# Tap matrices loaded instead of built, state rows moved whole, and idle products of ones in TensorE's planned waits

## The chip, the core and the metric

One core of a Trainium2 chip runs the program. The metric is the time of one execution in microseconds on the device; three runs of the kernel before are shown, and one further execution was profiled. An engine is called by its letters in the profile: PE is TensorE (PEld its weight loads), DVE VectorE, ACT ScalarE, POOL GpSimd, SP SyncE, which issues all DMA transfers of this kernel.

## What is computed

Two layers of a streaming encoder for 576 frames: 512 of a new stream and 64 of a running one with caches. Cut to what the change touches:

```
def trunk_layer(x, conv_state, k_past, v_past, ki_past, ...):
    h = x @ w_in
    a, g, q, k, v, qi, ki, wi = jnp.split(h, points, axis=-1)
    u = a * jax.nn.sigmoid(g)
    conv_out, new_conv = conv_mixer(u, conv_state, ...)
    ...
    mix = jnp.concatenate([conv_out, attn_out], axis=-1) @ w_o
    x = layer_norm(ALPHA * x + mix, ln1_g, ln1_b)
    gate, up = jnp.split(x @ w_gate_up, 2, axis=-1)
    x = layer_norm(ALPHA * x + (jax.nn.silu(gate) * up) @ w_down, ln2_g, ln2_b)
    return x, k, v, ki, new_conv
```

`conv_mixer` is a depthwise convolution of 31 taps with a layer norm and silu behind it; between it and the end come rope, indexer scores, a top-k and attention. `new_conv` is the last 30 rows of the convolution's input; they are an output (`conv_p` for the new stream, `conv_s` for the running one), and the rows of the running stream before it (`state_conv`) are an input.

## The kernel before, in words

The program is not written in the order in which it runs. Every operation is recorded by a `Plan` (lines 175 to 251) with a priority, an estimated cost and what it depends on. `schedule` (253 to 350) lays the operations out over the five engines by these costs, always the most urgent that can start; a tile gets a place in its pool when its first operation is laid out, and for some tags (`IN_TURN`, 156, `tap` and the wide PSUM tag `w` among them) in the order of recording. `issue` (352 to 362) then emits the list; each engine executes its part strictly in that order and waits where data is late. All instructions are emitted from line 362, so the profile shows that line for nearly all of them, and rows are told apart by the names of the tiles.

A layer begins with the input projection `w_in` in 18 tiles of 512 KB. A weight tile is loaded into `raw` (two buffers), split into two parts `whi` (ScalarE) and `wlo` (VectorE or GpSimd), and each product is made of three matmuls (`prod`). Rope sends its rows through DMA to exchange halves (`rope_s<-rope_h`).

The convolution works on four chunks of 128 channels. `glu` (720 to 735) writes the gated input of a chunk into `u`, eight phases of 80 columns; the four columns of state per phase come by a DMA from `st` (723), and the last columns of either stream go out by two DMAs straight from `u` (731, 732): runs of four floats. `convolve` (654 to 677) sends `u` to DRAM (`ud`) and back as `v` with another arrangement of partitions. Then, for each of eight phases, GpSimd builds a tap matrix `taps` of 128 x 640 from an identity (`eyes`) and the taps (`wv`), two buffers (664 to 667), and TensorE makes five float32 products of 76 columns with it (669 to 671); a float32 product shows as two instructions. The result is in a `wide` PSUM tile of two banks, of which there is one; VectorE reads it in two halves into `y` (673 to 676). The same wide tile takes the shift of the convolution's norm, the sums and spreads of all norms (`Moments`, 489 to 524) and the logits of the 64 running frames (926).

Indexer scores (`dots`), top-k on VectorE (`m`, `sel`) and attention (`qk`, `pp`, `po`) are interleaved with the convolution. Then follow `w_o` with a norm, and SwiGLU in four parts, where a Strassen-like scheme of seven products (`Seven`, 1076 to 1149) takes most tiles; its sums `s3`, `s4` use the tag `tap` too.

Of the kernel before, what the change touches and what calls it, by code (L numbers as in the profile page):

```python
# [49 lines left out]
PH = 8  # L50
# [7 lines left out]
CWID = PH * COUT  # L58

# [112 lines left out]
HOP, TABLE_LOAD, TABLE_LEAD = 0.2, 1.283, 0  # L172


class Plan:
# [175 lines left out]

    def issue(self):
        nc = self.tc.nc
        take = lambda v: v.real() if isinstance(v, View) else v
        with self.tc.manual_schedule():
            for op in self.schedule():
                for t in op.tiles.values():
                    if t.ap is None:
                        tag = f"{t.tag}.{t.place}"
                        t.ap = t.pool.tile(t.shape, t.dt, tag=tag, name=t.name, bufs=1)  # L360
                engine = getattr(nc, op.done[2])
                getattr(engine, op.method)(*map(take, op.args), **{k: take(v) for k, v in op.kw.items()})  # L362
# [3 lines left out]
def stream_step(ctx, tc, ins, outs):  # L366
# [21 lines left out]
    eyes = const.tile([P, CB], F32, name="eyes")  # L388
# [22 lines left out]
    def wide(name):  # L411
        return pw.tile([P, 2, 512], F32, tag="w", name=name)
# [20 lines left out]
    nc.sync.dma_start(eyes, ins["eyes"])  # L433
    nc.gpsimd.memset(ones, 1.0)
    nc.gpsimd.memset(bias0, 0.0)
# [53 lines left out]
    class Moments:  # L489
# [5 lines left out]
        def stats(self):  # L495
            m, tiles, count = self.m, self.tiles, self.count
            ps = wide("stats")
            for b, c in ((0, 496), (1, 504)):
                for i in range(tiles):
                    nc.tensor.matmul(ps[:m, 0, c + i:c + i + 1], self.s[b][:, i * m:(i + 1) * m], ones[:, 0:1],  # L500
                                     start=True, stop=True)
# [3 lines left out]
            nc.vector.tensor_scalar(nmu, ps[:m, 0, 496:496 + tiles], -1.0 / count, None, op0=OP.mult)  # L505
            nc.vector.tensor_mul(msq, nmu, nmu)
            nc.vector.scalar_tensor_tensor(rstd, ps[:m, 0, 504:504 + tiles], 1.0 / count, msq,
# [5 lines left out]
        def spread(self, b):  # L513

            m, tiles, n, dst = self.m, self.tiles, self.n, self.dst[b]
            per = tiles if tiles == 3 else tiles // 2
            ps = wide("spread")
            for i in range(tiles):
                nc.tensor.matmul(ps[:, i // per, (i % per) * m:(i % per + 1) * m],
                                 self.st[:m, b, i:i + 1].to_broadcast([m, P]), ident[:m, :m], start=True, stop=True)  # L520
# [122 lines left out]
    def layer(l):  # L643
# [10 lines left out]
        def convolve(c):  # L654
            wv = slot.tile([P, PH, CJ * PH], F32, tag="wv", name="wv")
            nc.sync.dma_start(wv, ins["cw"][l, c])
# [6 lines left out]
            for b in range(PH):  # L663
                sw = tmp("taps", "tap", CJ * P)
                shape = [P, CJ * PH, CB]
                nc.gpsimd.tensor_mul(sw.rearrange("p (a b) -> p a b", b=CB), eyes.unsqueeze(1).to_broadcast(shape),
                                     wv[:, b, :].unsqueeze(2).to_broadcast(shape))
                o = b % 4 * COUT
                for j in range(CJ):
                    nc.tensor.matmul(ps[:, b // 4, o:o + COUT], sw[:, j * P:(j + 1) * P], v[:, b, j:j + COUT],  # L670
                                     start=(j == 0), stop=(j == CJ - 1))
            y = slot.tile([P, PH, COUT], F32, tag=f"u{c}", name=f"y{c}")
            for h in range(2):
                nc.vector.tensor_add(y[:, 4 * h:4 * h + 4, :], ps[:, h, :4 * COUT].rearrange("p (b t) -> p b t", b=4),
# [12 lines left out]
        def conv_sums():  # L687
            def square(x):
                sq = tmp("csq", "tap", UW)[:, :CWID]
# [3 lines left out]
            for c in range(4):  # L693
                acc = cs[c]
                if c == 0:
                    shift = slot.tile([P, UW], F32, tag="u0", name="cshift")[:, :CWID]
                    ps = wide("cshift")
                    for h in range(2):
                        nc.tensor.matmul(ps[:, h, :CWID // 2], ones, acc[:, h * CWID // 2:(h + 1) * CWID // 2],
                                         start=True, stop=True)  # L700
                    nc.scalar.activation(shift.rearrange("p (a b) -> p a b", a=2), ps[:, :, :CWID // 2], AF.Copy,
                                         scale=-1.0 / P)
# [85 lines left out]
        wtok = small.tile([P, 32], F32, tag="wtok", name="wtok", bufs=1)  # L788
# [121 lines left out]
        def logits(t, u):  # L910
# [13 lines left out]
            else:  # L924
                g = u // 2
                ps = wide("qk").rearrange("p a b -> p (a b)")
# [10 lines left out]
        def values(t, u, pr):  # L937
# [8 lines left out]
            if t == 4:  # L946
                pn = bank("pp", "p")
                nc.tensor.transpose(pn[:NS, :P], pr[:, PAST:s], ident)
                ptn = tmp("ptn", "nmu", HT)[:, :P]
# [58 lines left out]
        nmu, rstd = [tmp(x, "tap", UW)[:, :CWID] for x in ("cnmu", "crstd")]  # L1008
# [29 lines left out]
        def sums_of_x():  # L1038
# [9 lines left out]
            for k in (0, 2):  # L1048
# [27 lines left out]
        class Seven:  # L1076

            def __init__(self, l, j, ops):
# [9 lines left out]
                s3, s4 = (tmp(x, "tap", CJ * P)[:, :n] for x in ("s3", "s4"))  # L1088
# [139 lines left out]
def _layout(x_prompt, x_sample, cache_k, cache_v, cache_k_idx, state_conv, w_in, conv_w, conv_b, conv_ln_g,  # L1228
# [53 lines left out]
    taps = taps.reshape(PH, CJ * PH, DEPTH, NCT, PH, CB).transpose(2, 3, 0, 5, 4, 1)  # L1282
    a["cw"] = taps.reshape(DEPTH, NCT, P, PH, CJ * PH)
    a["eyes"] = np.tile(np.eye(CB, dtype=np.float32), (PH, 1))
# [38 lines left out]
```

## Time and profile before

| | |
|---|---|
| median of 3 runs | 1572.07 us (1569.68 to 1573.81) |
| the profiled execution | 1578.27 us |
| its span, first to last instruction | 1576.5 us |
| mean granted clock of TensorE | 0.926 of 2.4 GHz |
| busy: PE, DVE, ACT, POOL | 1466.2, 1096.8, 721.0, 484.3 us |
| DMA moved | 125.12 MB in 87712 packets, 49441 of them under 512 B |

Layer 0 takes the first 820 us or so, layer 1 the rest. Busy times of engines overlap, so they don't add up to the span; the chain that ended last says whose time is the span's. A granted clock of 0.50 is the lower of TensorE's two levels (1.2 GHz), and a stretch with both shows a value between.

### The profile page before, as it was taken

What the parts mean: (1) busy time and instruction counts of PE and PEld (TensorE: products, weight loads), DVE (VectorE), ACT (ScalarE), POOL (GpSimd) and SP (SyncE); (2) the same over time, 40 slices, a digit from 0 to 9 for tenths busy, and PEclk for the clock granted to TensorE, in tenths of its full rate; (3) what the DMA queues carried; (4) which work ended last, traced back from release to release, by engine and by line L of the source; (5) the groups of instructions that cost most, each with busy time, mean ns of one, the idle gap of its engine ahead of it and who ended that gap; (6) DMA issues with size and microseconds to landing.
All of it is one profiled execution on the core that took longest, in us unless ns stands there. A gap on an engine that the chain in (4) does not pass through costs nothing.

```text
span 1576.5 us, 26565 instructions
## 1 busy us (share of the span) xinstructions
PE 1466.2 (93%) x10246; PEld 1427.4 (91%) x10246; DVE 1096.8 (70%) x2040; ACT 721.0 (46%) x1421; POOL 484.3 (31%) x413
## 2 busy tenths in 40 slices
PE   5799899898999999999996998989989999999996
PEld 5789888898899999999995988979979999999996
DVE  3359878456868668577764989764586785775875
ACT  3334344643635435346453434446364452552643
POOL 1030456333213203122611316533431141230343
PEclk9979959698999999999998997877989999999997
DMA  6625411011132222223327362200112222232221
GB/s 190 121 76 78 118 55 37 14 51 45 54 107 91 88 82 97 90 92 94 99 43 139 73 107 69 68 16 28 55 43 85 101 95 93 81 98 91 78 71 61
DMA packets 87712, 125.12 MB, mean 79 GB/s; under 512 B 49441, under 2 KB 55713, under 8 KB 87585
## 3 DMA queue, kind: packets, MB, share of 16 engines
q1 hardware_dynamic: 87584, 123.42, 28.2%
q8 instruction: 80, 1.31, 0.3%
q14 instruction: 48, 0.39, 0.1%
HBM read 108.81 MB, written 9.21 MB: 75 GB/s over the span
## 4 chain that ended last, share of the span: by engine, by line
PE 74%; DVE 13%; DMA 5%; ACT 3%; SPq 2%; issue 2%; POOL 1%; ACTq 0%; DVEq 0%; POOLq 0%
PE prod L362 30%; PE q L362 16%; PE r L362 8%; PE conv L362 5%; PE c L362 4%; PE po L362 3%; DVE X L362 3%; DMA ud<-u 2%; SPq L362 2%; DVE sel L362 2%; PE qk L362 2%; DVE wlo L362 2%; DVE rope_h L362 2%; PE pp L362 2%; PE dots L362 2%
## 5 line engine op out<-in xcount | busy, mean ns | idle before, releaser
L362 PE MATMUL prod<-XH,whi 128*128 128x288 f32 (+2 forms) x928 | 290.7, 319 | 45.6 <-ACT rope_h L362 25.4
L362 DVE TENSOR_TENSOR wlo<-raw,whi 128x512 fp32r<-128x512 f32 (+2 forms) x199 | 248.4, 1249 | 119.3 <-ACT whi L362 117.3
L362 ACT ACTIVATE whi<-raw 128x1024 fp32r<-128x1024 f32 (+2 forms) x206 | 183.0, 889 | 287.7 <-PE prod L362 174.3
L362 PE MATMUL prod<-XH,wlo 128*128 128x288 f32 (+2 forms) x928 | 290.3, 315 | 7.4 <-DVE wlo L362 7.4
L362 PE MATMUL prod<-XL,whi 128*128 128x288 f32 (+2 forms) x928 | 291.8, 316 | 2.8 <-DVE XL L362 2.7
L362 PEld LDWEIGHTS prod<-XH,whi 128*128 128x128 f32 (+1 forms) x928 | 183.3, 200 | 52.0 <-ACT rope_h L362 27.1
L362 PE MATMUL prod<-hl,whi 128*128 128x288 f32 x704 | 208.0, 296 | 0.2
L362 PE MATMUL prod<-hh,wlo 128*128 128x288 f32 x704 | 207.7, 296 | 0.0
L362 PE MATMUL prod<-hh,whi 128*128 128x288 f32 x704 | 207.0, 295 | 0.0
L362 PEld LDWEIGHTS prod<-XH,wlo 128*128 128x128 f32 (+1 forms) x928 | 182.1, 197 | 10.6 <-DVE wlo L362 8.4
L362 PEld LDWEIGHTS prod<-XL,whi 128*128 128x128 f32 (+1 forms) x928 | 183.8, 198 | 8.2 <-DVE XL L362 6.1
L362 ACT ACTIVATE whi<-s 128x512 fp32r<-128x512 f32 x160 | 96.4, 626 | 134.9 <-PE q L362 101.8
L362 DVE TENSOR_TENSOR wlo<-s,whi 128x512 fp32r<-128x512 f32 x158 | 107.3, 700 | 65.3 <-ACT whi L362 64.3
L362 PE MATMUL q<-XH,wlo 128*128 128x288 f32 x480 | 141.2, 295 | 1.5 <-DVE wlo L362 1.3
L362 PE MATMUL q<-XL,whi 128*128 128x288 f32 x480 | 141.4, 295 | 0.0
L362 PE MATMUL q<-XH,whi 128*128 128x288 f32 x480 | 141.3, 294 | 0.0
L362 PEld LDWEIGHTS prod<-hl,whi 128*128 128x128 f32 x704 | 132.1, 188 | 1.0 <-DVE hl L362 0.7
L362 PEld LDWEIGHTS prod<-hh,wlo 128*128 128x128 f32 x704 | 132.0, 188 | 0.1
L362 PEld LDWEIGHTS prod<-hh,whi 128*128 128x128 f32 x704 | 131.9, 188 | 0.2
L362 POOL TENSOR_TENSOR s<-raw 128x512 f32<-128x512 f32 x28 | 44.9, 1607 | 248.6 <-DVE wlo L362 210.6
L362 POOL TENSOR_TENSOR taps<-eyes,wv 128x640 f32<-128x640 f32 x64 | 87.4, 1369 | 91.1 <-PE conv L362 60.8
L362 DVE TENSOR_TENSOR X<-X,prod 128x288 f32<-128x288 f32 x120 | 53.1, 449 | 86.1 <-PE prod L362 85.5
(195 smaller groups left out, 3537.1 us busy)
## 6 DMA issues: line engine op xcount, KB each, us to landing
raw<-in_w_u SPq DMA_DIRECT2D x44, 512.0 KB, 3.2
raw<-in_w_g SPq DMA_DIRECT2D x44, 512.0 KB, 3.2
raw<-in_w_in SPq DMA_DIRECT2D x36, 512.0 KB, 4.3
raw<-in_w_d SPq DMA_DIRECT2D x48, 384.0 KB, 3.0
raw<-in_w_o SPq DMA_DIRECT2D x16, 512.0 KB, 3.3
raw<-in_w_d SPq DMA_DIRECT2D x16, 256.0 KB, 2.7
rope_s<-rope_h SPq DMA_DIRECT2D x48, 72.0 KB, 2.0
ud<-u SPq DMA_DIRECT2D x8, 320.0 KB, 9.6
```

Of the source, the lines that this page charges most:

```text
L362: getattr(engine, op.method)(*map(take, op.args), **{k: take(v) for k, v in op.kw.items()})
```

## The change

1. `convolve` loads each tap matrix (320 KB) from memory, where it now lies ready, instead of building it on GpSimd. The tag `tap` has three buffers instead of two; `eyes` and `wv` are gone. To make room, `nmu` has one buffer, `wtok` takes the slot of `qsm`, and `t4l` that of `sel2`.
2. The state rows come in and go out as whole rows of 32 floats; GpSimd copies them to and from `u`.
3. The wide tile is declared as 1024 columns in place of 2 x 512, and what was copied out of both banks in one instruction on ScalarE is copied in two.
4. After `schedule`, `filled` goes through the list again with another set of prices and reckons when each operation would start. Where TensorE would wait, it inserts products ones x ones (128 x 128, float32), 0.9 of the wait divided by 0.237 us of them, rounded down. They write columns 816 to 943 of whichever wide tile is current, which nobody reads, and are held back while an accumulation in the wide tile is open. With `FORCE` at 0.0 the second condition inserts none.

```diff
+SIGNAL, IDLE, FILL, CLOCK, FORCE, LATE = 0.04, (0.237, 0.213), 0.9, 3.4, 0.0, 1
...
+    def filled(self, order):
...
+        for op in order:
+            e = op.done[2]
+            t = free[e]
+            for w in op.waits:
+                if w.done[2] != e:
+                    t = max(t, ended[w.seq] + SIGNAL)
+                elif e != "tensor":
+                    t = max(t, ended[w.seq] + 0.02)
...
+            if op.method == "dma_start":
+                free[e] = t + op.generate
+                dma = max(dma, free[e] + 0.65) + op.nbytes / 300e3
+                end = dma + 1.2
+            elif e == "tensor":
+                cost, streamed = self.spacing(op)
+                now = free[e]
+                if not begun:
+                    now, begun = 1.0, True
+                n = int(FILL * (t - now) / IDLE[0])
+                while recent and recent[0][0] < now - CLOCK:
+                    act -= recent.pop(0)[1]
+                if act < FORCE * CLOCK and n < LATE:
+                    n += 1
+                for _ in range(n):
+                    out.append(None)
+                    recent.append((now, IDLE[1]))
+                    act += IDLE[1]
+                    now += IDLE[0]
+                t = max(t, now)
+                recent.append((t, streamed))
+                act += streamed
+                free[e] = t + cost
+                end = free[e] + 0.18
+            else:
+                cost = op.cost[e]
+                if e == "scalar":
...
+                else:
+                    x = t
+                    if e == "gpsimd" and op.method != "memset" or e == "vector" and self.two_read(op):
+                        if port[0] != e:
+                            x = max(x, port[1])
+                        port[:] = e, x + cost
+                    free[e] = x + cost
+                    end = free[e] + 0.09
...
+    def two_read(self, op):
+        return (op.method in ("tensor_add", "tensor_sub", "tensor_mul", "scalar_tensor_tensor")
+                and not any(v.tile.pool is p for v in op.args if isinstance(v, View) for p in self.psum))
+
+    def spacing(self, op):
+        n = op.args[0].columns()
+        if op.method == "transpose":
+            return 0.111, n / 2400
+        if n == 1:
+            return 0.16, 0.0
+        if F32R in (op.args[1].tile.dt, op.args[2].tile.dt):
+            return max(0.111, 0.0065 + 0.0004375 * n), n / 2400
+        return 2 * max(0.111, 0.0065 + 0.000875 * n), n / 600
...
     def issue(self):
...
-            for op in self.schedule():
+            t, cols, ones = self.filler
+            idle, due, group = t.pool.tile(t.shape, t.dt, tag=f"{t.tag}.0", name=t.name, bufs=1), 0, set()
+            for op in self.filled(self.schedule()):
+                if op is None:
+                    due += 1
+                while due and not group:
+                    nc.tensor.matmul(idle[:, cols], take(ones), take(ones), start=True, stop=True)
+                    due -= 1
+                if op is None:
+                    continue
+                if op.method == "matmul" and op.args[0].tile.tag == self.filler[0].tag:
+                    (group.discard if op.kw["stop"] else group.add)(op.args[0].idx.flat[0])
...
     def wide(name):
-        return pw.tile([P, 2, 512], F32, tag="w", name=name)
+        return pw.tile([P, 1024], F32, tag="w", name=name)
...
+    nc.filler = Held(pw.pool, [P, 1024], F32, "w", "idle", 1), slice(512 + WB, 512 + WB + P), ones
...
-            if tiles > per:
-                nc.scalar.activation(dst.rearrange("p (a b) -> p a b", a=2), ps[:, :, :n // 2], AF.Copy)
-            else:
-                nc.scalar.activation(dst, ps[:, 0, :n], AF.Copy)
+            for a in range(0, n, per * m):
+                nc.scalar.activation(dst[:, a:a + per * m], ps[:, a // (per * m) * 512:][:, :per * m], AF.Copy)
...
-            nmu, rstd = dst = [tmp(x, x, HT) for x in ("nmu", "rstd")]
+            nmu, rstd = dst = [tmp(x, x, HT, n) for x, n in (("nmu", 1), ("rstd", 2))]
...
         def convolve(c):
-            wv = slot.tile([P, PH, CJ * PH], F32, tag="wv", name="wv")
-            nc.sync.dma_start(wv, ins["cw"][l, c])
...
-                sw = tmp("taps", "tap", CJ * P)
-                shape = [P, CJ * PH, CB]
-                nc.gpsimd.tensor_mul(sw.rearrange("p (a b) -> p a b", b=CB), eyes.unsqueeze(1).to_broadcast(shape),
-                                     wv[:, b, :].unsqueeze(2).to_broadcast(shape))
-                o = b % 4 * COUT
+                sw = tmp("taps", "tap", CJ * P, 3)
+                nc.sync.dma_start(sw, ins["cw"][l, c, b])
+                o = b // 4 * 512 + b % 4 * COUT
...
         def glu(c, pg, pa):
-            nc.sync.dma_start(u[:, :, I_S:I_S + PADS], ins["st"][l, c])
+            row = small.tile([P, PH * PADS], F32, tag="cin", name="cin", bufs=1)
+            nc.sync.dma_start(row, ins["st"][l, c].rearrange("p s t -> p (s t)"))
+            nc.gpsimd.tensor_copy(u[:, :, I_S:I_S + PADS], row.rearrange("p (s t) -> p s t", s=PH))
...
-            nc.sync.dma_start(outs["conv_p"][l, c], u[:, :, I_S - PADS:I_S])
-            nc.sync.dma_start(outs["conv_s"][l, c], u[:, :, CIN - PADS:])
             us.append(u)
+            for name, i in (("conv_p", I_S - PADS), ("conv_s", CIN - PADS)):
+                row = small.tile([P, PH * PADS], F32, tag="cout", name="cout", bufs=2)
+                nc.gpsimd.tensor_copy(row.rearrange("p (s t) -> p s t", s=PH), u[:, :, i:i + PADS])
+                nc.sync.dma_start(outs[name][l, c].rearrange("p s t -> p (s t)"), row)
...
-        wtok = small.tile([P, 32], F32, tag="wtok", name="wtok", bufs=1)
+        wtok = slot.tile([P, 32], F32, tag="qsm", name="wtok")
...
-                            lo = slot.tile([P, HT], F32R, tag=("wv", "sel1")[i], name="t4l")
+                            lo = slot.tile([P, HT], F32R, tag=("sel2", "sel1")[i], name="t4l")
...
```

## Rows read from the trace of the kernel before

**Rows 1.** The page, parts 1 (busy us and share) and 4 (chain by engine).

```profile
PE 1466.2 (93%) x10246; PEld 1427.4 (91%) x10246; DVE 1096.8 (70%) x2040; ACT 721.0 (46%) x1421; POOL 484.3 (31%) x413
...
PE 74%; DVE 13%; DMA 5%; ACT 3%; SPq 2%; issue 2%; POOL 1%; ACTq 0%; DVEq 0%; POOLq 0%
```

**Rows 2.** The cores: span and mean granted clock.

```profile
core 0: 1576.5 us, clock 0.926
```

**Rows 3.** Windows: start:end length, busy PE PEld DVE ACT POOL, PEclk, DMA share, GB/s.

```profile
25.00:110.00 85.00, 71.89 (x418) 68.53 (x419) 37.61 (x53) 26.32 (x50) 16.59 (x12) 0.85 0.45 101
...
200.00:310.00 110.00, 100.45 (x596) 93.58 (x596) 77.92 (x180) 51.54 (x119) 55.21 (x45) 0.70 0.13 37
...
405.00:820.00 415.00, 411.94 (x3076) 408.82 (x3077) 302.31 (x486) 198.74 (x378) 115.40 (x98) 1.00 0.27 88
820.00:880.00 60.00, 45.00 (x257) 41.95 (x257) 30.73 (x44) 20.22 (x41) 15.87 (x11) 0.86 0.65 121
...
960.00:1100.00 140.00, 127.00 (x807) 119.62 (x806) 97.58 (x225) 71.90 (x157) 65.52 (x54) 0.77 0.14 40
```

**Rows 4.** Windows again, finer, of convolution and attention.

```profile
200.00:235.00 35.00, 33.42 (x170) 31.92 (x169) 25.19 (x65) 14.04 (x45) 18.30 (x17) 0.55 0.19 52
235.00:265.00 30.00, 29.06 (x244) 27.64 (x243) 25.94 (x66) 11.49 (x31) 15.79 (x14) 1.00 0.14 41
265.00:310.00 45.00, 37.96 (x187) 34.02 (x186) 26.79 (x51) 26.01 (x44) 21.12 (x15) 0.62 0.08 22
960.00:1000.00 40.00, 34.48 (x182) 33.42 (x180) 30.87 (x79) 17.41 (x46) 21.65 (x21) 0.62 0.18 55
1045.00:1085.00 40.00, 36.47 (x182) 34.52 (x183) 20.15 (x36) 24.99 (x42) 14.82 (x11) 0.57 0.04 14
95.00:113.00 18.00, 15.47 (x80) 15.20 (x80) 8.29 (x14) 2.96 (x9) 6.78 (x6) 0.62 0.07 16
```

**Rows 5.** The chain in order of time: start us, us, what.

```profile
44.80 10.76 DMA ud<-u
...
206.90 2.17 PE conv L362 x10
...
241.17 1.07 PE conv L362 x10
...
264.55 1.09 PE cshift L362 x4
...
823.12 18.46 DMA ud<-u
...
923.35 9.30 DMA ud<-u
```

**Rows 6.** Waits of PE: who waited for whom, us in total, times, longest.

```profile
PE prod L362 <- ACT rope_h L362: 25.4, 6, 6.7
PE qk L362 <- DVE mx L362: 16.2, 7, 4.6
...
PE conv L362 <- DVE y L362: 5.3, 7, 2.0
```

**Rows 7.** DMA issues: count, KB each, median us from issue to landing.

```profile
raw<-in_w_u SPq DMA_DIRECT2D x44, 512.0 KB, 3.2
...
yd<-y SPq DMA_DIRECT2D x8, 304.0 KB, 2.2
...
out_conv_p<-u SPq DMA_DIRECT2D x8, 16.0 KB, 8.0
out_conv_s<-u SPq DMA_DIRECT2D x8, 16.0 KB, 9.6
```

**Rows 8.** Groups of POOL: count, busy us, mean ns, idle before and its releasers.

```profile
L362 POOL TENSOR_TENSOR taps<-eyes,wv 128x640 f32<-128x640 f32 x64 | 87.4, 1369 | 91.1 <-PE conv L362 60.8 <-DMA u<-in_st 14.0 <-DMA wv<-in_cw 9.7
...
L362 POOL CAST qsm<-q 128x64 fp32r<-128x64 f32 x16 | 7.6, 492 | 12.6 <-DVE q L362 12.6
```

**Rows 9.** Groups of ACT, the same columns.

```profile
L362 ACT ACTIVATE cnmu<-spread 128x608 f32<-128x608 f32 x2 | 1.4, 677 | 7.7 <-PE spread L362 7.7
```

More of the change, by code (lines that the diff above doesn't have):

```diff
@@ L350, in schedule @@
         return order
+    def filled(self, order):
+        free, ended, held, out = dict.fromkeys(("tensor", "vector", "scalar", "gpsimd", "sync"), 0.0), {}, {}, []
+        dma, table, port, recent, act, begun = 0.0, None, ["", 0.0], [], 0.0, False
+        for op in order:
[6 more added lines that the diff above has]
+                    t = max(t, ended[w.seq] + 0.02)
+            for x in op.tiles.values():
+                last = held.get((id(x.pool), x.tag, x.place))
+                if last and last[0] is not x:
+                    t = max(t, last[1] + SIGNAL)
+            if op.method == "dma_start":
[25 more added lines that the diff above has]
+                if e == "scalar":
+                    if op.table not in (None, table):
+                        t += TABLE_LOAD
+                        table = op.table
+                    free[e] = t + cost
+                    end = free[e] + 0.1
+                else:
[6 more added lines that the diff above has]
+                    end = free[e] + 0.09
+            out.append(op)
+            ended[op.seq] = end
+            for x in op.tiles.values():
+                key = (id(x.pool), x.tag, x.place)
+                last = held.get(key)
+                held[key] = x, max(end, last[1]) if last and last[0] is x else end
+        return out
@@ L360, in issue @@
                         t.ap = t.pool.tile(t.shape, t.dt, tag=tag, name=t.name, bufs=1)
+                        if t.tag == self.filler[0].tag:
+                            idle = t.ap
                 engine = getattr(nc, op.done[2])
@@ L504, in stats @@
             nmu, rstd = st[:m, 0, :tiles], st[:m, 1, :tiles]
[L505 removed]
+            nc.vector.tensor_scalar(nmu, ps[:m, 496:496 + tiles], -1.0 / count, None, op0=OP.mult)
             nc.vector.tensor_mul(msq, nmu, nmu)
[L507 removed]
+            nc.vector.scalar_tensor_tensor(rstd, ps[:m, 504:504 + tiles], 1.0 / count, msq,
                                            op0=OP.mult, op1=OP.subtract)
@@ L688, in square @@
             def square(x):
-                sq = tmp("csq", "tap", UW)[:, :CWID]
+                sq = tmp("csq", "tap", CWID, 3)
                 nc.scalar.activation(sq, x, AF.Square)
@@ L698, in conv_sums @@
                     for h in range(2):
-                        nc.tensor.matmul(ps[:, h, :CWID // 2], ones, acc[:, h * CWID // 2:(h + 1) * CWID // 2],
+                        nc.tensor.matmul(ps[:, 512 * h:512 * h + WB], ones, acc[:, h * CWID // 2:(h + 1) * CWID // 2],
                                          start=True, stop=True)
-                    nc.scalar.activation(shift.rearrange("p (a b) -> p a b", a=2), ps[:, :, :CWID // 2], AF.Copy,
-                                         scale=-1.0 / P)
+                    for h in range(2):
+                        nc.scalar.activation(shift[:, h * WB:(h + 1) * WB], ps[:, 512 * h:512 * h + WB], AF.Copy,
+                                             scale=-1.0 / P)
                 eng = nc.vector if c == 3 else nc.gpsimd
@@ L925, in logits @@
                 g = u // 2
-                ps = wide("qk").rearrange("p a b -> p (a b)")
+                ps = wide("qk")
                 q = qsm[:, u * P:(u + 1) * P]
@@ L948, in values @@
                 nc.tensor.transpose(pn[:NS, :P], pr[:, PAST:s], ident)
-                ptn = tmp("ptn", "nmu", HT)[:, :P]
+                ptn = tmp("ptn", "nmu", HT, 1)[:, :P]
                 nc.scalar.activation(ptn[:NS], pn[:NS, :P], AF.Copy)
@@ L1007, in layer @@
         s1, s2 = conv_sums()
-        nmu, rstd = [tmp(x, "tap", UW)[:, :CWID] for x in ("cnmu", "crstd")]
+        nmu, rstd = [tmp(x, "tap", CWID, 3) for x in ("cnmu", "crstd")]
         mo = Moments(s1, s2, CC, CWID, PH, (nmu, rstd))
@@ L1087, in __init__ @@
                 s1, s2 = tmp("s1", "pt", CC), tmp("s2", "pt", CC)
-                s3, s4 = (tmp(x, "tap", CJ * P)[:, :n] for x in ("s3", "s4"))
+                s3, s4 = (tmp(x, "tap", CJ * P, 3)[:, :n] for x in ("s3", "s4"))
                 self.w = {}
@@ L1281, in _layout @@
                     taps[s, j, p] = conv_w[:, k]
-    taps = taps.reshape(PH, CJ * PH, DEPTH, NCT, PH, CB).transpose(2, 3, 0, 5, 4, 1)
-    a["cw"] = taps.reshape(DEPTH, NCT, P, PH, CJ * PH)
-    a["eyes"] = np.tile(np.eye(CB, dtype=np.float32), (PH, 1))
+    taps = taps.reshape(PH, CJ * PH, DEPTH, NCT, PH, CB).transpose(2, 3, 4, 0, 5, 1)
+    tiles_ = np.zeros((DEPTH, NCT, PH, PH, CB, CJ * PH, CB), np.float32)
+    for c in range(CB):
+        tiles_[:, :, :, :, c, :, c] = taps[:, :, :, :, c]
+    a["cw"] = tiles_.reshape(DEPTH, NCT, PH, P, CJ * P)
     half = HD // 2
```

13 lines of the change are left out of this document (6 added, 7 removed).

## The prediction

> **What bounds the kernel now.** I read the page first [rows 1]: TensorE is busy 93% of the span and holds 74% of the chain that ended last. Its granted clock is 0.926 on average over 1576.5 us [rows 2]. Then the windows by stage [rows 3]. In the first layer's SwiGLU stretch (405 to 820 us) TensorE is busy 411.9 of 415 us at clock 1.00, and the second layer's is alike: half the span, and this change can only spoil it. The other half is where time can be had, in two forms. TensorE idles, above all in the input projections (13.1 us of 25 to 110, 15.0 of 820 to 880). And it is busy at a low clock: 0.70 in 200 to 310, 0.77 in 960 to 1100, where convolution, top-k and attention are interleaved. The finer windows [rows 4] show stretches at 0.55 to 0.62, most of the time at the lower level (0.50 of full, 1.2 GHz), with TensorE nearly always busy, while 235 to 265 does the same kind of work at 1.00. The chain [rows 5] gives the price: ten tap-product instructions take 2.17 us at 206.90 (low) and 1.07 us at 241.17 (full). What TensorE did before the fall: it waited for other engines, up to 4.6 us at a time for VectorE's `mx` and up to 6.7 us for rope copies on ScalarE [rows 6].
>
> Low-clock time altogether: 1576.5 x (1 - 0.926) = 117 us is the most that the clock can return.
>
> **The change, part by part.**
>
> *Idle products.* They fill 0.9 of each wait of at least 0.26 us that the replay sees. None of this form is in the trace. The nearest row is `cshift`, also ones times something in float32: four instructions in 1.09 us for two products of 304 columns, 0.27 us each instruction; ten 76-column instructions took 1.07 us, 0.11 each [rows 5]. For 128 columns that bounds a product of two instructions by 0.21 and 0.55 us; by columns, 0.27 x 128/304 = 0.115 an instruction, I take 0.23 us at full clock, 0.46 at half. The replay costs TensorE at full clock, so it sees as waiting both the real idle time (1576.5 - 1466.2 = 110 us) and what a full clock would free (up to 117 us): at most 0.9 x 227 / 0.23 = 890 products. I reckon with 700, 161 us of added TensorE time meant to lie in waits.
>
> What they return is the clock. For each stretch of [rows 4] but the one at 1.00 I take the smaller of the low-clock loss, span x (1 - clock), and the time in which VectorE is free, since a faster TensorE next meets VectorE's top-k and softmax work: 200 to 235 min(15.8, 9.8) = 9.8; 265 to 310 min(17.1, 18.2) = 17.1; 960 to 1000 min(15.2, 9.1) = 9.1; 1045 to 1085 min(17.2, 19.9) = 17.2; 95 to 113 min(6.8, 9.7) = 6.8. Sum 60. TensorE is busy 84 to 95% of those stretches, so the chain there is mostly but not only its own, and I take three quarters, 45 us. The remaining loss, 117 - 72 = 45 us, lies in short pieces around waits on DMA and in the final normalisation, where VectorE ends the chain; a third, 15 us. **Clock: -60 us**; ends 0 and -117. After it, VectorE is late next in 200 to 265 and 960 to 1035.
>
> Products that fall where TensorE has work cost 0.23 us each. The order on each engine is fixed, so an error of the replay stays local; I take 60 misplaced, **+14 us**; ends 0 and 161.
>
> *State rows.* Sixteen stores `out_conv_p`, `out_conv_s` and eight loads `u<-in_st` move 16 KB each in 16-byte runs. The stores take 8.0 and 9.6 us to land, against 2.2 us for `yd<-y` with 304 KB [rows 7]. What is queued behind them is worse: `ud<-u`, of 320 KB, lands after 10.8, 18.5 and 9.3 us on the chain [rows 5], though a transfer of its size needs 2.2. The excess is 8.6 + 16.3 + 7.1 = 32 us, and SyncE's own queue stood still for weights and rope shuffles meanwhile. TensorE idled 13.1 + 15.0 = 28 us in those two stages, part of it for other reasons (rope copies on ScalarE). **-20 us**; ends 0 and -32. Each row transfer gets a POOL copy of 128 x 32; the nearest copy, 128 x 64, takes 0.49 us [rows 8], so 24 of them are below 12 us, covered by what POOL loses below. They stand on the path only where `u` waits for its state row, which is loaded long before; the stores have nobody waiting.
>
> *Tap matrices.* POOL loses 64 multiplications, 87.4 us [rows 8]. It waited 60.8 us for TensorE to release a buffer in those: building was hidden behind TensorE, POOL holds 1% of the chain, so by itself this returns nothing; where POOL and VectorE delay one another it may give up to 8 us, not taken. In place come 64 loads of 320 KB on SyncE's queue, 21 MB, less 8 small loads of `wv`. A load of 304 KB lands in 2.2 us and one of 512 KB in 3.2 [rows 7]; I take 2.5 plus 0.4 for issue. With three buffers one group may be refilled every 2.9 / 3 = 0.97 us against 1.07 us for its products at full clock: just hidden. A tap load waits on SyncE for TensorE to release its buffer, and weight loads and rope shuffles stand behind it. If each tap load also had a weight load ahead of it (3.2 us), it would be (2.9 + 3.2) / 3 - 1.07 = 0.96 us a group, 61 us for 64: the far end. The near end is 0. At the very start three tap loads need nothing and may precede a weight: 0.98 MB, about two weight loads, at most 6.4 us by their landing of 3.2 us one after the other; they overlap, so I take **+4 us.**
>
> *The rest* I cost at nothing: `nmu` with one buffer is reused a half later, after its eight additions; `wtok` and `t4l` sit in slots whose other use is far away; spreads copied in two pieces add a fixed cost on ScalarE, six times at most the 0.68 us of the whole copy [rows 9], under 4 us even if uncovered.
>
> **Sum:** -60 - 20 + 14 + 4 = -62 us. The profiled execution took 1578.3 us, 6.2 over the median 1572.1; against the median, 1572 - 62 = **1510 us**.
>
> One rule of the Trainium skill speaks against the change. In the trace TensorE waited 5.3 us in 7 pieces for VectorE to read a convolution result, 0.76 us each, and 16.2 us in 7 pieces for `mx`, 2.3 each, 4.6 at most [rows 6]. The Trainium skill, page "PSUM — Partial Sum Buffer", section "PSUM bank collisions raise a hardware error", says to guard PSUM by bank and quadrant, not by address. The idle products write columns 816 to 943 of the wide tile, its second bank, which VectorE or ScalarE reads 22 times (8 half results of the convolution, 2 shifts, 4 spreads, 8 sample logits). By that rule a product there must wait for the reader although no address is shared, and the sum would be 17 us (0.76 each) to 101 us (4.6 each) worse; without it the sum stands. No run here shows it yet.
>
> **The rivals.**
> 1. *The products do not hold the clock*, or the replay finds few waits: half-clock stretches stay, idle time only changes its name. For it: from 200 to 235 us TensorE was busy 33.4 of 35 us and stayed at 0.55 [rows 4]. Against: the dense products of the SwiGLU stretch hold 1.00 [rows 3]. Then 1572 - 20 + 4 = 1556 us.
> 2. *Slower: the products stand in the way.* Place: attention and convolution, where waits are short and VectorE's times vary. Price 0.23 us each on an in-order engine. Without misplacement the gain is 76 us, so it turns at 330 of 700, 47%. At two thirds misplaced, 107 - 76 gives 1603 us. Against it: the replay's prices agree with rows here (0.11 us a pass), and waits shorter than 0.26 us get none.
> 3. *The product waits for a reader of its bank*, by the rule above: at the 2.3 us of a mean wait on `mx`, 22 x 2.3 = 51 us, 1561 us; at 4.6, slower than before.
> 4. *Tap loads late in SyncE's queue:* +61 in place of +4 less what was hidden, 1567 us, about no change. For it: SyncE's queue already waits most of the span.
>
> **How the numbers follow.** Forecast 0.62; rival 1 0.12; rival 2 0.12; rival 3 0.07; rival 4 0.07. A measurement of this kernel can tell about 0.3%, 5 us, from no change. Faster: 0.62 + 0.12 + most of 3 and some of 4, 0.81. Same 0.06. Slower: rival 2 and the ends of 3 and 4, 0.13. The forecast alone spans 1470 to 1550. The range goes down to the whole clock loss returned and nothing else, 1572 - 117 = 1455, and up to 1580, which takes in rivals 1, 4 and most of 3 and leaves out rival 2.
>
> **What would show it.** Right: granted clock in the convolution and attention stretches near 1.00, tap products at 0.11 us an instruction throughout; `ud<-u` landing in 2 to 3 us; several hundred small float32 products on ones; POOL near 410 us; the SwiGLU stretches as long as before. Wrong: the clock still 0.5 in those stretches; products of ones within the SwiGLU stretches; PE waits named after the ones product or after tap loads; the span unchanged with a full clock, which would say that VectorE was the bound.

## The result, and the profile after

The changed kernel takes 1518.17 us in the median of 4 runs (1514.44 to 1523.97) against 1572.07 us; the ratio is 0.9661 with an interval of 0.9624 to 0.9699, 3.4% faster. The prediction said 1510 us, 1455 to 1580. The profiled execution took 1523.97 us, its span 1522.2 us, the longest of the four. Runs of one kernel differ by about 1% and go with the clock (the change 1514 us at 0.976, 1524 at 0.968); ratios here and below leave out runs over 1.5% above their kernel's fastest, medians don't.

The page, its parts 1 (busy us and share), 2 (granted clock in 40 slices) and 4 (chain by engine):

```profile
PE 1485.7 (98%) x10908; PEld 1455.4 (96%) x10908; DVE 1070.3 (70%) x2049; ACT 720.0 (47%) x1427; POOL 388.0 (25%) x364
...
PEclk9999997999999999999998996989999999999998
...
PE 81%; DVE 11%; ACT 3%; issue 2%; DMA 2%; POOL 1%; SPq 0%; DVEq 0%; ACTq 0%; POOLq 0%
```

The cores, span and mean granted clock:

```profile
core 0: 1522.2 us, clock 0.968
```

Against [rows 1, 2]: TensorE has 662 more instructions (331 products of ones, two each) and 19.5 us more busy time in a span 54.3 us shorter. The clock rose from 0.926 to 0.968, so the low-clock time fell from 117 to 1522.2 x 0.032 = 49 us. The DMA's share of the chain went from 5% to 2%, SyncE's from 2% to nothing. POOL fell from 484.3 to 388.0 us; I had written "near 410".

The windows by stage, columns as in [rows 3]. All times after lie earlier, so stages are compared and not equal clock times:

```profile
25.00:110.00 85.00, 83.75 (x546) 80.82 (x545) 51.53 (x99) 36.38 (x75) 11.70 (x15) 0.94 0.48 144
...
200.00:310.00 110.00, 106.08 (x762) 100.02 (x763) 65.44 (x146) 60.54 (x120) 34.54 (x29) 0.91 0.20 62
...
400.00:800.00 400.00, 398.86 (x2983) 396.46 (x2982) 282.84 (x460) 184.54 (x352) 95.57 (x95) 1.00 0.29 95
800.00:860.00 60.00, 56.89 (x357) 53.85 (x356) 46.04 (x98) 30.55 (x67) 6.81 (x7) 0.91 0.48 141
...
940.00:1060.00 120.00, 114.89 (x836) 108.19 (x836) 72.29 (x169) 64.84 (x134) 28.25 (x24) 0.91 0.23 70
```

Two things changed. The input projection (25 to 110) is dense: 83.75 us busy where it was 71.89. And convolution and attention (200 to 310) run at clock 0.91 where it was 0.70. SwiGLU is as before.

What TensorE waited for (us in total, times, longest):

```profile
PE qk L460 <- DVE mx L460: 9.4, 6, 2.4
PE conv L460 <- DVE y L460: 4.1, 6, 1.2
...
PE stats L447 <- DVE st L460: 1.3, 3, 0.5
PE conv L460 <- DMA taps<-in_cw: 1.1, 3, 0.8
...
PE spread L447 <- ACT nmu L460: 0.6, 1, 0.6
...
PE spread L447 <- ACT rstd L460: 0.4, 1, 0.4
```

The DMA issues (count, KB each, median us from issue to landing):

```profile
taps<-in_cw SPq DMA_DIRECT2D x64, 320.0 KB, 3.2
ud<-u SPq DMA_DIRECT2D x8, 320.0 KB, 3.2
...
out_conv_p<-cout SPq DMA_DIRECT2D x8, 16.0 KB, 2.2
out_conv_s<-cout SPq DMA_DIRECT2D x8, 16.0 KB, 2.2
```

The largest wait of [rows 6], 25.4 us of `prod` for ScalarE's `rope_h`, is gone altogether, and `mx` fell from 16.2 to 9.4 us. The state stores land in 2.2 us where they took 8.0 and 9.6, and `ud<-u` lands in 3.2 us where its median before was 9.6:

```profile
ud<-u SPq DMA_DIRECT2D x8, 320.0 KB, 9.6
```

In the lines of the kernel after, L447 is the line that issues products of ones, L460 all other operations.

### The profile page after: what moved, and what is told of

It reads as the page before. It is cut to its first block, busy times and chain, and to the rows that moved or that the text cites. A ratio compares the mean times of both kernels' runs of the same rounds, so it can differ in the third digit from the quotient of the medians.

```text
span 1522.2 us, 27875 instructions
## 1 busy us (share of the span) xinstructions
PE 1485.7 (98%) x10908; PEld 1455.4 (96%) x10908; DVE 1070.3 (70%) x2049; ACT 720.0 (47%) x1427; POOL 388.0 (25%) x364
## 4 chain that ended last, share of the span: by engine, by line
PE 81%; DVE 11%; ACT 3%; issue 2%; DMA 2%; POOL 1%; SPq 0%; DVEq 0%; ACTq 0%; POOLq 0%
PE prod L460 33%; PE q L460 17%; PE r L460 8%; PE conv L460 5%; PE c L460 4%; PE po L460 3%; PE dots L460 2%; DVE X L460 2%; DVE rope_h L460 2%; DVE sel L460 2%; PE spread L460 1%; DVE m L460 1%; PE qk L460 1%; PE pp L460 1%; PE spread L447 1%
## 5 line engine op out<-in xcount | busy, mean ns | idle before, releaser
L460 DVE TENSOR_TENSOR wlo<-raw,whi 128x1024 fp32r<-128x1024 f32 (+2 forms) x198 | 246.7, 1247 | 88.6 <-ACT whi L460 86.9
L460 ACT ACTIVATE whi<-raw 128x1024 fp32r<-128x1024 f32 (+2 forms) x206 | 182.8, 889 | 251.7 <-PE prod L460 174.1
L460 PE MATMUL prod<-XL,whi 128*128 128x288 f32 (+2 forms) x928 | 280.7, 304 | 0.4 <-DVE XL L460 0.3
L460 PE MATMUL prod<-XH,wlo 128*128 128x288 f32 (+2 forms) x928 | 278.7, 302 | 0.0
L460 PE MATMUL prod<-XH,whi 128*128 128x288 f32 (+2 forms) x928 | 276.9, 304 | 0.3
L460 PE MATMUL prod<-hl,whi 128*128 128x288 f32 x704 | 207.9, 296 | 0.0
L460 PE MATMUL prod<-hh,wlo 128*128 128x288 f32 x704 | 207.5, 296 | 0.0
L460 PE MATMUL prod<-hh,whi 128*128 128x288 f32 x704 | 207.5, 296 | 0.0
L460 PEld LDWEIGHTS prod<-XL,whi 128*128 128x128 f32 (+1 forms) x928 | 173.6, 187 | 3.6 <-DVE XL L460 1.5
L460 PEld LDWEIGHTS prod<-XH,whi 128*128 128x128 f32 (+1 forms) x928 | 171.9, 187 | 3.6 <-ACT whi L460 0.9
L460 PEld LDWEIGHTS prod<-XH,wlo 128*128 128x128 f32 (+1 forms) x928 | 173.3, 187 | 1.6
L460 ACT ACTIVATE whi<-s 128x512 fp32r<-128x512 f32 x160 | 96.4, 626 | 143.7 <-PE q L460 111.0
L460 DVE TENSOR_TENSOR wlo<-s,whi 128x512 fp32r<-128x512 f32 x158 | 107.0, 699 | 65.8 <-ACT whi L460 61.8
L460 PE MATMUL q<-XH,wlo 128*128 128x288 f32 x480 | 141.2, 295 | 1.3 <-DVE wlo L460 1.3
L460 PE MATMUL q<-XH,whi 128*128 128x288 f32 x480 | 141.5, 295 | 0.0
L460 PE MATMUL q<-XL,whi 128*128 128x288 f32 x480 | 141.4, 295 | 0.0
L460 PEld LDWEIGHTS prod<-hl,whi 128*128 128x128 f32 x704 | 132.1, 188 | 0.7 <-POOL hl L460 0.2
L460 PEld LDWEIGHTS prod<-hh,whi 128*128 128x128 f32 x704 | 131.9, 188 | 0.2
L460 PEld LDWEIGHTS prod<-hh,wlo 128*128 128x128 f32 x704 | 132.0, 188 | 0.0
L460 DVE TENSOR_TENSOR X<-X,prod 128x288 f32<-128x288 f32 x120 | 53.5, 451 | 80.3 <-PE prod L460 79.5
L460 PE MATMUL conv<-v,taps 128*128 128x76 f32 x640 | 97.0, 302 | 5.4 <-DVE y L460 4.1
L460 PEld LDWEIGHTS conv<-v,taps 128*128 128x128 f32 x640 | 92.3, 220 | 8.0 <-DVE y L460 5.3
```

## The experiments

The change has three parts: products of ones, whole state rows, loaded taps. Three kernels have one part alone, a fourth has all but the products. All have the small edits (`nmu`, `wtok`, `t4l`, spreads copied in pieces). The kernel before, measured beside them, took 1573.13 us.

**no_idle**: the change with no product inserted.

```diff
-                n = int(FILL * (t - now) / IDLE[0])
+                n = 0
```

(`LATE` is 0 as well.)

> The changed kernel without one idle product; tap loads and whole state rows stay. Theory (the products give the clock back, and that is most of the gain): the granted clock falls back to about 0.93 and the time to about 1556 us. Rival (the freed DMA queues give most of the gain, the products only fill idle time): within 5 us of the changed kernel's 1518 us.

Measured 1531.42 us (1518.71 to 1540.26), ratio 0.9747 (0.9668 to 0.9826), profiled clock 0.935: between theory and rival. Most of the gain is there without any product.

**only_idle**: products alone; taps built on POOL from `eyes` and `wv`, state rows in 16-byte runs.

```diff
-                nc.sync.dma_start(sw, ins["cw"][l, c, b])
+                nc.gpsimd.tensor_mul(sw.rearrange("p (a b) -> p a b", b=CB), eyes.unsqueeze(1).to_broadcast(shape),
+                                     wv[:, b, :].unsqueeze(2).to_broadcast(shape))
...
-            nc.sync.dma_start(row, ins["st"][l, c].rearrange("p s t -> p (s t)"))
-            nc.gpsimd.tensor_copy(u[:, :, I_S:I_S + PADS], row.rearrange("p (s t) -> p s t", s=PH))
+            nc.sync.dma_start(u[:, :, I_S:I_S + PADS], ins["st"][l, c])
...
+            nc.sync.dma_start(outs["conv_p"][l, c], u[:, :, I_S - PADS:I_S])
+            nc.sync.dma_start(outs["conv_s"][l, c], u[:, :, CIN - PADS:])
```

> Taps built on GpSimd with two buffers and state rows in 16-byte runs as before; only the idle products are added (and the small edits that make room). Theory: about 1525 us, clock about 0.96, since the waits on DMA are filled too. Rival: about 1560 us, because the transfers stay late whatever TensorE does in the meantime.

Measured 1575.3 us, ratio 1.0026 (0.9998 to 1.0053): no gain, though the clock rose from 0.926 to 0.966; neither theory nor rival had that. So a higher clock and no shorter time go together here, and the question becomes what the products cost.

**only_rows**: whole state rows alone (taps built, no products); its edits are those above, without the rows' part.

> Taps built on GpSimd, no idle products; only the state rows move as whole rows. Theory: 20 us from the input projections, about 1552 us, with ud<-u landing in 2 to 3 us. Rival (the rows are the main gain): below 1540 us. Against both: about 1572 us if the late transfers were covered by other work.

Measured 1524.13 us, ratio 0.9693 (0.9645 to 0.9741), clock 0.940: 49 us, nine tenths of the change's gain, from 24 transfers of 16 KB. I had given the rows 20 us and called 32 the most.

**only_taps**: taps loaded, the rows in runs, no products.

> No idle products, state rows in 16-byte runs; only the tap matrices are loaded, with three buffers. Theory: between 1568 and 1580 us, since building was hidden behind TensorE and the loads are just hidden. Rival: below 1560 us, if GpSimd's building delayed VectorE and TensorE more than the waits of the profile say; or above 1590 us, if the loads hold up the weights on SyncE's queue.

Measured 1566.51 us, ratio 0.9968 (0.9935 to 1.0001): 7 us, near the limit of what can be told. The three parts alone give -49, +2 and -7 us, -54 together, and the whole change gives -54. That they add up so well is chance: rows and taps together (no_idle) give -42 and not -56.

The next four (kernel before 1572.64 us) take one part away from the change, or alter the products.

**built_taps**: the change with built taps (the POOL lines above).

> The changed kernel with the taps built on GpSimd again (two tap buffers); whole rows and idle products stay. Theory after the first four runs (rows give nearly all, products about 13 us on top, loads next to nothing): 1511 to 1522 us. Rival (loading is what makes the products pay, since it frees GpSimd and so VectorE): 1524 us or more, as with the rows alone.

Measured 1534.72 us, ratio 0.9771 (0.9733 to 0.9810): 17 us slower than the change, at a higher clock, 0.977, and 11 us slower than only_rows, its twin without products. The theory's time is missed; this one is on the rival's side. The replay sees more waits when POOL builds taps: 402 products in place of 331, most of the additional ones in the convolution (111 there in place of 55; two instructions each):

```profile
L447 PE MATMUL conv<-ones 128*128 128x128 f32 x222 | 34.1, 298 | 0.7 <-DVE y L460 0.7
```

**old_rows**: the change with the rows in 16-byte runs (the last lines of the diff above).

> The changed kernel with the state rows in 16-byte runs again; loaded taps and idle products stay. Theory: about 45 us over the changed kernel, 1560 to 1568 us, with ud<-u late again and the first dense products at 25 us or later. Rival (the products and the loads make up for late transfers): below 1545 us.

Measured 1560.56 us, ratio 0.9935 (0.9896 to 0.9974): 42 us slower than the change, as the theory had it.

With these two, all eight combinations of the three parts are measured. The ratios to the kernel before:

```
                             no products           products
built taps, rows in runs     1                     1.0026 (only_idle)
loaded taps, rows in runs    0.9968 (only_taps)    0.9935 (old_rows)
built taps, whole rows       0.9693 (only_rows)    0.9771 (built_taps)
loaded taps, whole rows      0.9747 (no_idle)      0.9661 (the change)
```

Whole rows gain in every pair, 35 to 49 us by the medians. Products cost 2 and 11 us beside built taps and return 6 and 13 beside loaded ones; the difference between the two cases is 1.1% of the time, with an uncertainty of about 0.6% by the intervals of the eight ratios. Loaded taps in turn come out at -7 and +7 us without products, about nothing, and at -15 and -17 us with them. So products and loaded taps pay only together. Where the products' cost goes shows in the chain that ended last: behind the first 104 us, products of ones hold 57 us of it in only_idle and in built_taps, 39 in old_rows and 41 in the change.

**one_column**: each product multiplies one column in place of 128, at the same places.

```diff
-                    nc.tensor.matmul(idle[:, cols], take(ones), take(ones), start=True, stop=True)
+                    nc.tensor.matmul(idle[:, cols.start:cols.start + 1], take(ones), take(ones[:, 0:1]), start=True, stop=True)
```

> The changed kernel with every idle product cut to one column: as many instructions in the same places, each with its weight load, next to nothing streamed. Theory (what the products give is the clock): clock back to about 0.935 and time to that of the kernel without products, about 1531 us. Rival (they act by keeping TensorE occupied, or by the order they impose): clock about 0.97 and 1518 us.

Measured 1600.76 us (1583.16 to 1618.56), ratio 1.0141 (1.0081 to 1.0201), profiled clock 0.928: the clock as in the theory, the time far above both. By the two ratios the same 662 instructions cost 62 us over no products when they don't hold the clock. Groups of TensorE, products only (count, busy us, mean ns), of the change:

```profile
L447 PE MATMUL spread<-ones 128*128 128x128 f32 x286 | 38.2, 279 | 0.9 <-ACT nmu L460 0.6 <-ACT rstd L460 0.4
L447 PE MATMUL conv<-ones 128*128 128x128 f32 x110 | 18.7, 314 | 0.0
...
L447 PE MATMUL qk<-ones 128*128 128x128 f32 x104 | 13.9, 293 | 0.0
```

The same groups of this kernel:

```profile
L447 PE MATMUL spread<-ones 128*128 128x1 f32 x286 | 38.2, 256 | 0.9 <-ACT nmu L460 0.6 <-ACT rstd L460 0.4
...
L447 PE MATMUL conv<-ones 128*128 128x1 f32 x110 | 22.8, 321 | 0.0
L447 PE MATMUL qk<-ones 128*128 128x1 f32 x104 | 20.0, 323 | 0.0
```

A product of one column takes TensorE as long as one of 128: in both kernels the starts of successive instructions lie 0.11 us apart at full clock and 0.21 us at half. (The groups of the one-column kernel hold more instructions at half clock, so the equal 38.2 us for 286 is in part chance.) So products of ones don't get cheaper by narrowing them, and without the clock this kernel shows no return of them.

**force50**: a version that might be better: the planner also puts a product ahead of an instruction where the TensorE work that it has planned lately falls under half (`FORCE` 0.0 in the change, 0.5 here), wait or no wait.

> The changed kernel with FORCE at 0.5: one more product ahead of each operation where the replay counts less than half of the recent time streamed, wait or no wait. Theory (stretches that stay at half clock still cost 10 to 20 us in each layer): clock 0.98 or more and 1500 to 1512 us. Rival (VectorE and the softmax chain set the pace there, and forced products stand in the way): clock up, time 1520 us or more.

Measured 1509.32 us (1507.13 to 1516.21), ratio 0.9620 (0.9589 to 0.9652), clock 0.988. It is the fastest kernel of the study and beats the one before clearly; its interval overlaps that of the change, so that it beats the change too is likely but not settled.

The last three (kernel before 1578.14 us) ask where the rows' gain comes from and whether fewer products do as well.

**rows_in**: as only_rows, but only the 8 loads are whole; the 16 stores go in runs.

> As the kernel with whole rows alone (1524 us), but only the state loads are whole rows; the stores go out in 16-byte runs. Theory (the stores in front of ud<-u cost most, the loads about 10 us at the start of the first layer, where the first weights stand behind them): 1556 to 1564 us, first dense products at about 17 us in place of 25. Rival (the loads are nearly all of it): below 1535 us.

Measured 1571.38 us, ratio 0.9957 (0.9932 to 0.9982): 7 of the 49 us; the other 42 come with the stores. What SyncE's queue waited for in this kernel (us in total, times, longest):

```profile
SPq L460 <- DMA ud<-u: 45.7, 6, 9.2
```

What TensorE waited for in it:

```profile
PE prod L460 <- ACT rope_h L460: 26.5, 6, 6.2
```

Its DMA issues:

```profile
ud<-u SPq DMA_DIRECT2D x8, 320.0 KB, 10.0
...
out_conv_p<-u SPq DMA_DIRECT2D x8, 16.0 KB, 8.3
out_conv_s<-u SPq DMA_DIRECT2D x8, 16.0 KB, 10.0
```

And the queue's wait in only_rows, then in the kernel before:

```profile
SPq L460 <- DMA ud<-u: 3.9, 8, 1.0
```

```profile
SPq L362 <- DMA ud<-u: 43.4, 6, 8.7
```

With the stores in runs SyncE's queue stands 45.7 us for `ud<-u` (43.4 us before the change), with whole stores 3.9 us. Behind it stand the rope shuffles: the first goes out at 61.26 us in rows_in and at 48.81 in only_rows. VectorE's rope then comes late (ScalarE's copies of `k` waited 15.7 us for it, in only_rows 1.9), so do ScalarE's `rope_h` copies, and TensorE's `prod` waits 26.5 us for those, a wait that only_rows doesn't have at all.

One thing else changes with the whole stores, their place in SyncE's queue. The first issues of rows_in (start us, us):

```profile
37.94 0.66 SPq L460 DMA_DIRECT2D out_conv_p<-u  x1
38.69 0.62 SPq L460 DMA_DIRECT2D out_conv_s<-u  x1
...
40.22 0.42 SPq L460 DMA_DIRECT2D ud<-u  x1
```

And of only_rows:

```profile
38.28 0.33 SPq L460 DMA_DIRECT2D ud<-u  x1
39.41 0.34 SPq L460 DMA_DIRECT2D out_conv_p<-cout  x1
39.80 0.45 SPq L460 DMA_DIRECT2D out_conv_s<-cout  x1
```

In runs, the two stores of a chunk are queued ahead of its `ud<-u` in all eight chunks; as whole rows they wait for POOL's copies, and in six of eight chunks `ud<-u` goes first. That whole rows by themselves are enough shows where one still goes 0.4 us ahead of `ud<-u`: that lands in 2.2 us (only_rows, at 860.29) and 3.0 us (the change, at 108.89), against 9.2 to 19.7 right behind two stores in runs (rows_in and the kernel before). Whether stores in runs, moved behind `ud<-u`, would gain as much was not tried.

**force_only**: `FILL` 0.0 and `FORCE` 0.5, so no product in planned waits, only forced ones.

> The changed kernel with FILL at 0 and FORCE at 0.5: no product for a wait as such, one ahead of an operation where the replay counts less than half of the recent time streamed. Theory (two in three of the products for waits cost TensorE time, what pays is the clock): far fewer products, clock 0.96 or more and 1500 to 1512 us. Rival (the clock needs the waits filled): clock below 0.95 and 1520 us or more.

Measured 1515.31 us, ratio 0.9616 (0.9584 to 0.9647), profiled clock 0.972: as good as force50 with 161 products in place of 372.

**fill50f50**: `FILL` and `FORCE` both 0.5.

> The changed kernel with FILL at 0.5 and FORCE at 0.5, between the last one and the forced kernel of 1509 us. Theory: about half as many products for waits, clock 0.97 to 0.99, 1500 to 1510 us. Rival (products for waits cost nothing in this plan): clock lower and 1510 us or more.

Measured 1524.11 us, ratio 0.9656 (0.9626 to 0.9687), profiled clock 0.972, above the theory's 1510: filling the waits by half does not help, and the three settings can't be told apart.

## Where the products' time went

In a profiled execution span is TensorE's busy time plus its idle time, and busy time is that of products (L447) plus that of all other work. Between a kernel with products and its twin without, the three terms can be read off the pages and the product groups (us):

```
kernel - twin            span   products   other work    idle    clock
after - no_idle          -4.0     +95.2       -62.9     -36.3    0.935 -> 0.968
only_idle - before       -3.6    +118.8       -80.0     -42.4    0.926 -> 0.966
built_taps - only_rows   +2.5    +116.8       -73.5     -40.8    0.940 -> 0.977
one_column - no_idle    +56.8    +114.5       -17.2     -40.5    0.935 -> 0.928
force50 - no_idle       -19.2    +111.2       -95.4     -35.0    0.935 -> 0.988
force_only - no_idle     -6.1     +77.3       -87.7      +4.3    0.935 -> 0.972
fill50f50 - no_idle      +3.3    +101.0       -82.0     -15.7    0.935 -> 0.972
old_rows - only_taps     -6.3     +96.3       -61.2     -41.4    0.933 -> 0.967
```

For the first line: 1485.7 - 95.2 = 1390.5 us of other work against 1453.4 in no_idle; 1522.2 - 1485.7 = 36.5 us idle against 1526.2 - 1453.4 = 72.8. (The medians of these two lie 13 us apart, the profiled executions 4.) Products took 95 us; 36 us of idle time went for it, 59 us was not covered by that. The chain gives a lower figure, the 41 us above; part of the products may fill time that the faster clock freed, which this sum books as not covered. Other work got 63 us shorter. The low-clock time fell from 1526.2 x 0.065 = 99 to 49 us, so 50 of the 63 are the clock's; one_column, with 17 us less of other work at a lower clock, says that the remainder isn't (ends of pipelined matmuls are modelled, so time next to a product can be booked to either).

Where they stand shows why. Both spans are cut at the same instructions (the first `dots`, `qk`, `cshift`, `qk<-kp` and `q` of a layer). The products of the change alone, by stretch (length, TensorE busy us and count, PEclk, DMA share, GB/s):

```profile
0.00:103.90 103.90, 16.08 (x116) 0.95 0.59 187
...
164.00:222.00 58.00, 7.30 (x50) 1.00 0.58 173
...
255.70:376.90 121.20, 18.54 (x136) 0.97 0.14 49
376.90:703.60 326.70, 0.99 (x6) 1.00 0.28 93
...
906.60:977.40 70.80, 11.41 (x60) 0.81 0.47 142
...
1012.30:1131.20 118.90, 17.21 (x136) 1.00 0.14 50
```

All work in two stretches of no_idle (columns as in [rows 3]):

```profile
164.30:242.40 78.10, 72.92 (x388) 70.47 (x387) 49.73 (x127) 25.28 (x72) 9.75 (x11) 0.61 0.45 128
...
270.30:392.70 122.40, 110.91 (x767) 105.74 (x766) 76.22 (x151) 69.65 (x131) 48.60 (x40) 0.92 0.15 48
```

The 16 us at the start fill a real wait for the first weights and neither cost nor return time, though 15 us of the chain are booked to them: the stretch is 103.9 us long with them and 104.2 without. From the first `qk<-kp` to the SwiGLU (255.7 to 376.9) TensorE got 18.5 us of products where no_idle had 122.4 - 110.9 = 11.5 us idle; the clock rose from 0.92 to 0.97 and the stretch got 1.2 us shorter. The gain is in the first layer's convolution: 7.3 us of products, clock 0.61 to 1.00, 78.1 to 58.0 us; the next stretch (222.0 to 255.7) got 5.8 us longer. The second layer's stretch went the other way, 61.7 us in no_idle and 70.8 in the change. The change's chain there (start us, us, what):

```profile
911.53 4.45 PE conv L447 x28
915.98 1.74 PE conv L460 x16
...
927.78 2.05 PE conv L460 x10
...
933.56 2.05 PE conv L460 x10
...
957.42 1.07 PE conv L460 x10
```

And its windows, columns as in [rows 3]:

```profile
240.00:260.00 20.00, 20.00 (x102) 19.23 (x102) 5.94 (x16) 11.93 (x19) 9.77 (x6) 0.54 0.00 1
...
925.00:945.00 20.00, 20.00 (x98) 20.00 (x97) 11.54 (x26) 4.51 (x17) 1.88 (x3) 0.50 0.45 151
```

Fourteen products (28 instructions) in a row stand on the chain at 911.53, more follow, and the clock still falls: ten tap products take 2.05 us at 927.78 and 1.07 at 957.42. In 925 to 945 TensorE has no idle time at all and runs at 0.50; in 240 to 260 (statistics, spreads, small attention products) likewise at 0.54. A plan that fills waits has nothing to fill there. The forced products of force50 do reach these places; the windows of that kernel:

```profile
860.00:940.00 80.00, 75.24 (x586) 73.74 (x585) 72.16 (x187) 31.55 (x71) 25.93 (x23) 0.98 0.48 142
940.00:1060.00 120.00, 115.57 (x909) 109.39 (x909) 74.41 (x157) 65.17 (x130) 42.33 (x36) 1.00 0.22 64
```

There the second layer's convolution stretch takes 60.5 us, 10 less than in the change and about as long as without any product.

## Why the prediction came out right, and what in it did not

The total is right, 54 us of gain where 62 was forecast. But that is luck in good part: the products were to return 46 us net (-60 + 14) and return 13, the rows were to return 20 and return 42, the tap loads were to cost 4 and return 17 (each part taken out of the change by itself), and the errors offset one another. The sum also took the parts to be independent; they aren't, and the three figures add to more than the whole.

**Clock, -60: right in size for TensorE's own work.** The low-clock time fell by 50 us against no_idle and by 68 against the kernel before, and the bound of 117 us was not reached, because the clock still falls, as in 925 to 945, where there is no wait to fill. How much of it would have reached the span without the products' cost can't be read off: only the net is measured.

**Misplaced products, +14: the step that failed first.** I took 700 products and "60 misplaced" without a row behind the 60, on the ground that the replay's prices agree with rows. There are 331, each of 95.2 / 331 = 0.29 us where I took 0.23, and of their 95 us 41 stand on the chain behind the start, while 59 (62%) is not covered by idle time. The reason that I gave, that an error of the replay stays local, was not enough: the replay put 68 products, 18.5 us, into a stretch where no_idle had 11.5 us idle. That the waits between small instructions are short, near the price of one product, is my reading of it and was not tried. Rival 2 priced this and put its turning point at 47% misplaced; with built taps that point was reached (only_idle, 1.0026 alone; built_taps, 11 us slower than only_rows), with loaded taps it was not. In the change the products' net is 13 us by the medians of no_idle and the change, whose intervals of the ratio overlap.

**State rows, -20: mis-sized; 42 in the change, 35 to 49 in the four pairs.** The mechanism was right (stores in short runs delay the `ud<-u` behind them; it lands in 3.2 us, forecast 2 to 3), though I did not see that the stores would also move behind it. But I bounded the term by 32 us, the excess of the three `ud<-u` pieces on the chain. I put the waits of `prod` for `rope_h` aside as "other reasons (rope copies on ScalarE)". They were the same reason: those 25.4 us [rows 6] vanish in only_rows and stay in rows_in. The row that would have told it was the queue's own list of waits, `ud<-u` 43.4 us in 6 pieces before the change, which I named only as "stood still".

**Tap loads, +4: about right without products, wrong with them.** Without products they come out at -7 and +7 us, beside the products at -15 and -17. Landing takes 3.2 us where I took 2.5, but three buffers cover most of it: TensorE waited 1.1 us for taps, and the chain holds 8.4 us of tap loads in two pieces, so rival 4 fell. The 17 us go with the products on the chain: built_taps has 71 more of them (116.8 against 95.2 us of product time) and 16 us more of them on the chain. That the loads would take waits out of the replay's plan was in no term.

**Rival 1** (the products don't hold the clock) fell as put: 0.968. one_column is that rival made real, at a ratio of 1.0141, about 1594 us rather than 1556, since the products then still have to be paid. **Rival 3** (a product waits for the reader of its bank) cost next to nothing: in the change products waited 1.3 + 0.6 + 0.4 = 2.3 us for readers, and none of them for `y` or `mx`. The Trainium skill, page "PSUM — Partial Sum Buffer", section "PSUM bank collisions raise a hardware error", asks for guarding by bank, which made me price up to 101 us; the run shows that here such guarding, as far as it takes place, costs 2.3 us.

Of the signs I had named: tap products at 0.11 us an instruction hold only in part (1.07 us for ten at 957.42, 2.05 at 927.78); SwiGLU is unchanged, 326.5 us from the first `q` to the last before and 326.7 after, though three products fell into it (0.99 us); "several hundred small products" is right.

## What to carry to other kernels

Before adding work to hold a clock, measure what the work itself takes: compare a version with it and one without by busy time of the added work, busy time of the rest and idle time, since a higher granted clock beside products alone proved worth nothing here (0.926 to 0.966 with no shorter time). When a small transfer lands late, look at what the queue does behind it and who waits for that, several engines on; the wait's name on TensorE (`rope_h`) was three steps away from its cause (16-byte runs in a store). And a kernel whose total comes out as forecast still needs its parts run singly and in pairs: errors of 33 us on the products' net, 22 on the rows and 21 on the taps hid in this one, and the pairs showed that loaded taps and products pay only together.

## What the runs showed of the hardware that I had not expected

- Sixteen stores of 16 KB, in 16-byte runs and ahead of a 320 KB transfer on the same queue, cost about 42 us of 1572: they land in 8 to 10 us where whole rows land in 1.9 to 2.5, and the transfer takes 10.0 us in the median of rows_in in place of 3.2. The loads in the same runs cost little (7 us with the small edits).
- A float32 product of ones takes the same time with 1 column as with 128 (0.11 us from start to start at full clock, both), so the price by columns that I used (0.115) was near by chance.
- TensorE ran at 0.50 for 20 us without any idle time in the records (925 to 945); what it did in the ten microseconds before was small tap and attention products and products of ones, with three waits of 0.3 to 0.8 us.
